# One hand-set order from w_out's last row tiles to w_up's first columns in a hybrid decoder layer on one Trainium2 core

## The chip, the cores and the metric

The kernel runs on one core of a Trainium2 chip. The metric is device time in microseconds of one execution, the median of several. The core has a matrix engine (TensorE, PE in the profile; PEld is its weight load), a vector engine (VectorE, DVE), a scalar engine (ScalarE, ACT), a GpSimd engine (POOL), and a queue engine (SyncE, SP) that issues most transfers. Each engine works through its own instructions in the order fixed when the kernel is built, and engines wait for one another by semaphores. Matmuls write to PSUM, eight banks of 128 partitions by 512 float32; the rest of the on-chip data lies in SBUF.

## The reference, cut to what matters

A decoder layer on 256 tokens with model width 2048, in float32:

```python
mix = hybrid_mixer(rmsnorm(h, norm_mix_pre), w_in, ..., w_out)   # ends in y_mix (256 x 4096) @ w_out
h = h + rmsnorm(mix, norm_mix_post)
ff = squared_relu_mlp(rmsnorm(h, norm_mlp_pre), w_up, w_down)    # relu(u @ w_up)^2 @ w_down
h = h + rmsnorm(ff, norm_mlp_post)
```

The place that the change touches is the seam of the two halves: the last products with w_out, the norm of their result over all 2048 columns, the residual sum, u of the second norm (transposed, since a matmul contracts over partitions), and the first 512 columns of u @ w_up.

## The kernel before, in words

**Tiles.** Tokens come in two tiles of 128 (t = 0 and 1), matrices in column blocks of 512 (NB). A weight tile is two blocks of 128 rows by 512 columns (KB = 2, 512 KB), and "k" counts such pairs: w_out has 16, w_up 8. Precision comes from splitting each float32 operand in two parts that the matmul takes: `split` (lines 132 to 138) makes hi on ACT (L135, or L137 with a scale for each row) and lo = source - hi on DVE (L136, L138). A product of row tiles is then three matmuls for each block of rows: hi times hi, hi times the weights' lo, lo times hi (L233 to L235). One weight tile on one tile of tokens is so six matmuls; the text calls that a row tile.

**Buffers.** `fetch` loads a weight tile through SP's queue into a ring of four raw buffers (RAWS); `parts` takes hi and lo from a ring of five (BUFS). `weights` fetches and splits ahead of the matmuls, at high priority. `fetch_next` also uses the place of u's second part, `ub`, as raw buffers while u isn't needed, and `in_place_of_u` lends that of the first, `ua`, to the sums of the seven-product scheme below.

**w_out.** y_mix @ w_out has four column blocks, n = 0 to 3, done in two units of two blocks (`unit`). Some pairs of k are done with seven products instead of eight (`seven`), whose sums `combine_new` puts together. What is left of the unit is plain row tiles, for the last four k (11, 13, 14, 15) first of block 2, both tiles of tokens for each k, then of block 3. In block 3 the tokens of t = 1 lag one k behind (LAG_OUT = 1). `mixed` takes a finished block from PSUM: adds it to what the sums gave (L804), squares it on ACT for the norm (L806), and multiplies by the norm's weights (L807). `done` does that for block 3 and puts `residual(t)` in the line of waiting work, from which `pump` takes a step between row tiles.

**The seam.** `residual` computes the norm's factor (`scale_of`: a sum on DVE, L766, and a power on POOL, L767), then for each of the four column blocks adds mw * factor to h (L817), transposes the block on PE in four pieces of 128 (L822) and splits the transposed pieces into u (L137 and L138). Then it squares h (L830) and computes the next norm's factor, rmlp. The first block of w_up is a plain product of row tiles (`gemm_tokens`, LAG_UP = 1, line 901), since the next norm's factor isn't known yet; `first_hidden` applies it afterwards. `over_partitions` (L491 to L493) spreads the factor for the other blocks of w_up, which are computed transposed (`gemm_features`, L333 and L336).

**Order.** Within an engine a list scheduler picks at build time, among the instructions that it holds ready in its own timeline, the one of highest priority; `tc.high_priority` raises it (weights by AHEAD, the residual's steps by twice that), otherwise what was written earlier goes first. `tc.manual_schedule` keeps the instructions written under it in that order on every engine. Kernel before uses it for the first product of the kernel (`first_block`, lines 425 to 470), at the highest priority; the squares of x (L423) numbered 5 to 7 are written behind that stretch.

Of the kernel before, what the change touches and what calls it, by code (L numbers as in the profile page):

```python
# [10 lines left out]
F32 = mybir.dt.float32  # L11
F32R = mybir.dt.float32r
BF16 = mybir.dt.bfloat16
# [3 lines left out]
P = 128  # L17
S = 256
# [24 lines left out]
AHEAD = 1_000_000  # L43
BUFS = 5
RAWS = 4
LAG_OUT = 1
LAG_UP = 1
LAG_DOWN = 3
WARM = 6
STAY = 4  # L50
# [23 lines left out]
def hymba_layer(ctx: ExitStack, tc: tile.TileContext, x, norm_mix_pre, w_in, conv_w, conv_b, dt_bias, a_log,  # L74
# [22 lines left out]
    def u(k):  # L97

        return us[k // SUMS][:, k % SUMS]
# [32 lines left out]
    def split(hi, lo, src, scale=None):  # L132

        if scale is None:
            return (nc.scalar.activation(hi, src, AF.Copy),  # L135
                    nc.vector.tensor_tensor(lo, src, hi.bitcast(F32), op=ALU.subtract))  # L136
        return (nc.scalar.activation(hi, src, AF.Copy, scale=scale),  # L137
                nc.vector.scalar_tensor_tensor(lo, src, scale, hi.bitcast(F32), op0=ALU.mult, op1=ALU.subtract))  # L138
# [49 lines left out]
    def weights(src, k0, c0, fetch=fetch):  # L188

        with tc.high_priority(offset=AHEAD):  # L190
            raw = fetch(src, k0, c0)
            hi, lo = parts()
            if fetch is fetch_next:
                split_in_line(hi, lo, raw)
                return hi, lo
            line.clear()
            with ExitStack() as order:
                while behind:
                    order.enter_context(tc.issue_after(behind.pop().ins))
                split(hi, lo, raw)  # L200
        return hi, lo
# [11 lines left out]
    def drain():  # L213
        while waiting:
            pump()

    def row_tiles(src, c0, ks, acc, acts, first=True, last=True, lag=0, at_end=None, pumps=1, fetch=fetch):


        held = {}  # L220
        n = len(ks)
        for i in range(n + lag):
            if i < n:
                held[i] = weights(src, ks[i] * KB, c0, fetch)
            for t, at in ((0, i), (1, i - lag)):
                if not 0 <= at < n:
                    continue
                hi, lo = held[at]
                ts = slice(t * P, (t + 1) * P)
                for j in range(KB):  # L230
                    a_h, a_l, r = acts(ks[at] * KB + j)
                    begin, end = first and at == 0 and j == 0, last and at == n - 1 and j == KB - 1
                    nc.tensor.matmul(acc[t], a_h[:, r, ts], hi[:, j], start=begin, stop=False)  # L233
                    nc.tensor.matmul(acc[t], a_h[:, r, ts], lo[:, j], start=False, stop=False)  # L234
                    nc.tensor.matmul(acc[t], a_l[:, r, ts], hi[:, j], start=False, stop=end)  # L235
                if at == n - 1 and at_end:
                    at_end(t, acc[t])
            pump(pumps)
# [68 lines left out]
    def unit(src, n, order, last, acc, more, combine, lag=0, at_end=(None, None), pumps=1, first=True):  # L307


        cols = (n * NB, (n + 1) * NB)  # L310
        sevens = [k for k, by_seven in order if by_seven]
        for i, (k, by_seven) in enumerate(order):
            if i + 1 < len(order) and order[i + 1][1]:
                sums_of_acts(order[i + 1][0])
            if by_seven:
                seven(src, *cols, k, acc, more, k == sevens[0], k == sevens[-1])
            else:
                for b in range(2):
                    row_tiles(src, cols[b], [k], acc[b::2], part, first and i == 0, False, pumps=pumps,
                              fetch=fetch_next)  # L320
            if k == sevens[-1]:
                combine(more)
        for b in range(2):
            row_tiles(src, cols[b], last, acc[b::2], part, False, True, lag if b else 0, at_end[b], pumps,
                      fetch=fetch if b else fetch_next)

    def features():
        return [bank().rearrange("p (b s) -> p b s", b=2) for _ in range(4)]
# [10 lines left out]
    def gemm_features(src, c0):  # L339


        acc = features()
        for k0 in range(0, NK, KB):
            hi, lo = weights(src, k0, c0)
# [419 lines left out]
    def scale_of(dst, sums, some, t):  # L764
        m = cp.tile([P, 1], F32, name="mean", bufs=2)
        nc.vector.tensor_scalar(m, sums[:, t, 3:4], some, 1.0 / D, op0=ALU.add, op1=ALU.mult)  # L766
        nc.gpsimd.tensor_tensor(dst[:, t:t + 1], m, half[:, 0:1], op=ALU.pow)  # L767
# [4 lines left out]
    def columns(n):  # L772
        return slice(n * NB, (n + 1) * NB)
# [25 lines left out]
            nc.vector.tensor_tensor(mw[:, 1, b], mw[:, 1, b], u, op=ALU.subtract)  # L799

    def mixed(n, t, acc):
        cs = columns(n)
        with tc.high_priority(offset=2 * AHEAD):
            nc.vector.tensor_tensor(mw[:, t, cs], acc, mw[:, t, cs], op=ALU.subtract if n % 2 else ALU.add)  # L804
            junk = hp.tile([P, NB], BF16, name="junk", bufs=2)
            nc.scalar.activation(junk, mw[:, t, cs], AF.Square, accum_out=ssq[:, t, n:n + 1])  # L806
            nc.vector.tensor_mul(mw[:, t, cs], mw[:, t, cs], wpost[n])  # L807

    def residual(t):

        ts = slice(t * P, (t + 1) * P)
        with tc.high_priority(offset=2 * AHEAD):
            scale_of(rm, ssq, first3[t], t)
        for n in range(4):
            cs = slice(n * NB, (n + 1) * NB)
            with tc.high_priority(offset=2 * AHEAD):
                nc.vector.scalar_tensor_tensor(h[:, t, cs], mw[:, t, cs], rm[:, t:t + 1], h[:, t, cs],  # L817
                                               op0=ALU.mult, op1=ALU.add)
                p = bank() if n % 2 else psmall()
                for f in range(4):  # L820
                    k = 4 * n + f
                    nc.tensor.transpose(p[:, f * P:(f + 1) * P], h[:, t, k * P:(k + 1) * P], ident)  # L822
                for f in range(4):
                    k = 4 * n + f
                    split(u(k)[:, 0, ts], u(k)[:, 1, ts], p[:, f * P:(f + 1) * P], w_mlp[:, k:k + 1])
            yield
        for n in range(4):
            cs = slice(n * NB, (n + 1) * NB)
            junk = hp.tile([P, NB], BF16, name="junk", bufs=2)
            nc.scalar.activation(junk, h[:, t, cs], AF.Square, accum_out=ssh[:, t, n:n + 1])  # L830
        scale_of(rmlp, ssh, sums_but_last(ssh, t), t)

    def done(t, acc):
        if t == 0:
            new_u()
        mixed(3, t, acc)
        waiting.append(residual(t))

    in_place_of_u()
    acc = [bank() for _ in range(2 * NT)]  # L840
# [20 lines left out]
    more = [psmall(), bank(), psmall(), bank()]  # L861

    def whole(n):
        return lambda t, a: mixed(n, t, a)

    def order_of(ks, by_seven):
        return [(k, k in by_seven) for k in ks]
# [4 lines left out]
        load_wpost(norm_mix_post, n)  # L872
    acc, more = more, acc

    def third(t, a):
        mixed(2, t, a)
        first3.append(sums_but_last(ssq, t))

    first3 = []
    unit(w_out, 2, order_of((0, 1, 6, 2, 9, 3, 12, 5, 4, 7, 8, 10), (6, 9, 12, 4, 8)), (11, 13, 14, 15), acc, more,  # L880
         lambda x: combine_new(2, x), LAG_OUT, (third, done), 2)


    def hidden(k, r):
        nc.scalar.activation(r, r, AF.Square)
# [96 lines left out]
```

## Time and profile before

| what | value |
|---|---|
| time, median of 3 runs | 1501.83 us (1501.44 to 1502.44) |
| time of the profiled execution | 1501.53 us |
| its span, first to last instruction | 1499.8 us |
| PE busy | 1483.3 us, 99% of the span, 7674 instructions |
| DVE busy | 1025.2 us, 68% |
| ACT busy | 795.9 us, 53% |
| POOL busy | 58.0 us, 4% |
| DMA | 283.15 MB, mean 189 GB/s |
| mean granted clock of PE | 0.998 |

A timeline row reads: start in us from the span's start, duration, engine, line, operation, what is written <- what is read, shapes and count; in brackets the idle time just before it and what ended that. A row with a count over 1 merges neighbours. Matmuls are pipelined, so one of 0.39 us can follow the one before after 0.23. Tile names: hi and lo are parts of weights; ah and al (attention), sh and sl (SSD) are the parts of y_mix; ua and ub those of u; acc and ps are PSUM; mw is the mixer's result, rmix the norm's factor, h the residual stream.

### The profile page before, as it was taken

How to read it: one execution, taken by the hardware profiler on the slowest of the kernel's cores; microseconds unless marked ns; L12 is line 12 of the kernel's file. 1: busy time of each engine (PE TensorE's matmuls, PEld its weight loads, DVE VectorE, ACT ScalarE, POOL GpSimd, SP SyncE). 2: the span in 40 equal slices, each digit the busy share in tenths (PEclk: the TensorE clock that was granted, in tenths of full speed). 3: DMA queues.
4: the chain of work that ended last, by engine and by line, in shares of the span. 5: the costliest groups of instructions: out<-in, count | busy, mean ns of one | idle time of the engine just before them, and what ended most of it. 6: DMA issues, size and time to landing. Idle time of an engine off the chain costs nothing.

```text
span 1499.8 us, 20349 instructions
## 1 busy us (share of the span) xinstructions
PE 1483.3 (99%) x7674; PEld 1267.0 (84%) x7674; DVE 1025.2 (68%) x1498; ACT 795.9 (53%) x1111; POOL 58.0 (4%) x73
## 2 busy tenths in 40 slices
PE   9999999999999999999989999999999999999997
PEld 8888888888888888888878888888888888888886
DVE  6988797886555565688977656644444665688886
ACT  7574665464545454555656545534444554555552
POOL 0002200220000000000000000000000000000101
PEclk9999999999999999999999999999999999999999
DMA  7665666555655655665555666555556666656662
GB/s 270 199 201 180 183 183 195 172 167 172 179 169 172 179 169 177 209 244 201 195 174 175 183 193 186 184 195 195 192 191 197 191 186 193 187 196 203 205 210 98
DMA packets 148707, 283.15 MB, mean 189 GB/s; under 512 B 11408, under 2 KB 14336, under 8 KB 148352
## 3 DMA queue, kind: packets, MB, share of 16 engines
q1 hardware_dynamic: 143312, 272.37, 58.3%
q10 hardware_dynamic: 5296, 9.48, 1.9%
q8 instruction: 60, 0.98, 0.3%
q14 instruction: 39, 0.32, 0.1%
HBM read 279.68 MB, written 2.13 MB: 188 GB/s over the span
## 4 chain that ended last, share of the span: by engine, by line
PE 94%; DVE 3%; DMA 2%; issue 1%; ACT 0%; SPq 0%; POOL 0%; POOLq 0%; DVEq 0%; ACTq 0%
PE acc L333 29%; PE acc L336 15%; PE acc L233 12%; PE acc L235 12%; PE acc L234 12%; PE ps L234 1%; PE ps L235 1%; PE ps L233 1%; PE acc L304 1%; PE acc L305 1%; PE acc L303 1%; DVE lo L136 1%; PE ps L654 1%; DMA raw<-in_w_in_dram 1%; PE ps L304 0%
## 5 line engine op out<-in xcount | busy, mean ns | idle before, releaser
L136 DVE TENSOR_TENSOR lo<-raw,hi 128x1024 fp32r<-128x1024 f32 (+1 forms) x466 | 570.7, 1226 | 395.1 <-ACT hi L135 392.7
L135 ACT ACTIVATE hi<-raw 128x1024 fp32r<-128x1024 f32 (+1 forms) x466 | 491.0, 1055 | 517.5 <-PE acc L333 240.5
L333 PE MATMUL acc<-ua,hi 128*128 128x512 f32 x1240 | 333.8, 399 | 0.7 <-DVE ua L138 0.7
L333 PEld LDWEIGHTS acc<-ua,hi 128*128 128x128 f32 x1240 | 217.8, 189 | 34.3 <-DVE ua L138 0.9
L333 PE MATMUL acc<-ub,hi 128*128 128x512 f32 x744 | 205.5, 397 | 0.0
L336 PEld LDWEIGHTS acc<-ua,lo 128*128 128x128 f32 x1240 | 182.0, 189 | 21.0
L336 PE MATMUL acc<-ua,lo 128*128 128x256 f32 x1240 | 187.3, 281 | 0.0
L333 PEld LDWEIGHTS acc<-ub,hi 128*128 128x128 f32 x744 | 127.3, 189 | 16.2 <-issue 0.2
L336 PEld LDWEIGHTS acc<-ub,lo 128*128 128x128 f32 x744 | 114.3, 189 | 15.8
L336 PE MATMUL acc<-ub,lo 128*128 128x256 f32 x744 | 118.2, 281 | 0.0
L233 PE MATMUL acc<-hi,sh 128*128 128x512 f32 x280 | 110.1, 393 | 0.0
L235 PE MATMUL acc<-hi,sl 128*128 128x512 f32 x280 | 109.1, 390 | 0.0
L234 PE MATMUL acc<-lo,sh 128*128 128x512 f32 x280 | 109.1, 390 | 0.0
L233 PE MATMUL acc<-hi,ah 128*128 128x512 f32 x264 | 102.8, 389 | 0.0
L235 PE MATMUL acc<-hi,al 128*128 128x512 f32 x264 | 102.8, 389 | 0.0
L234 PE MATMUL acc<-lo,ah 128*128 128x512 f32 x264 | 102.8, 389 | 0.0
L233 PE MATMUL acc<-hi,ua 128*128 128x512 f32 x180 | 71.3, 396 | 0.3 <-ACT ua L137 0.3
L235 PE MATMUL acc<-hi,ua 128*128 128x512 f32 x180 | 70.2, 392 | 0.4 <-DVE ua L138 0.4
L234 PE MATMUL acc<-lo,ua 128*128 128x512 f32 x180 | 70.4, 391 | 0.0
L135 ACT ACTIVATE hi<-ub 128x1024 fp32r<-128x1024 f32 x48 | 50.4, 1058 | 37.5 <-PE acc L235 13.6
L136 DVE TENSOR_TENSOR lo<-ub,hi 128x1024 fp32r<-128x1024 f32 x48 | 58.3, 1222 | 12.1 <-ACT hi L135 11.5
L235 PEld LDWEIGHTS acc<-hi,sl 128*128 128x128 f32 x280 | 52.6, 188 | 11.0
(300 smaller groups left out, 1903.9 us busy)
## 6 DMA issues: line engine op xcount, KB each, us to landing
raw<-in_w_in_dram SPq DMA_DIRECT2D x190, 512.0 KB, 3.6
raw<-in_w_up_dram SPq DMA_DIRECT2D x128, 512.0 KB, 3.8
raw<-in_w_down_dram SPq DMA_DIRECT2D x104, 512.0 KB, 4.3
raw<-in_w_out_dram SPq DMA_DIRECT2D x40, 512.0 KB, 4.2
ub<-in_w_out_dram SPq DMA_DIRECT2D x24, 512.0 KB, 4.6
ub<-in_w_down_dram SPq DMA_DIRECT2D x24, 512.0 KB, 5.0
bc<-acs_d ACTq DMA_DIRECT2D x8, 512.0 KB, 4.4
xs<-in_x_dram SPq DMA_DIRECT2D x8, 256.0 KB, 6.4
```

Source lines behind the costliest of these rows:

```text
L135: return (nc.scalar.activation(hi, src, AF.Copy), nc.vector.tensor_tensor(lo, src, hi.bitcast(F32), op=ALU.subtract))
L136: nc.vector.tensor_tensor(lo, src, hi.bitcast(F32), op=ALU.subtract))
L233: nc.tensor.matmul(acc[t], a_h[:, r, ts], hi[:, j], start=begin, stop=False)
L234: nc.tensor.matmul(acc[t], a_h[:, r, ts], lo[:, j], start=False, stop=False)
L235: nc.tensor.matmul(acc[t], a_l[:, r, ts], hi[:, j], start=False, stop=end)
L303: nc.tensor.matmul(dst, a_h, hi[:, j], start=own and first, stop=False)
L304: nc.tensor.matmul(dst, a_h, lo[:, j], start=False, stop=False)
L305: nc.tensor.matmul(dst, a_l, hi[:, j], start=False, stop=own and last)
L333: nc.tensor.matmul(acc[f], hi[:, j, f * P:(f + 1) * P], u(k0 + j), start=k0 + j == 0, stop=False, skip_group_check=True)
L336: nc.tensor.matmul(acc[f][:, 0], lo[:, j, f * P:(f + 1) * P], u(k0 + j)[:, 0], start=False, stop=k0 + j == NK - 1, skip_group_check=True)
L654: nc.tensor.matmul(p[:, c, r], bc[:, r, c * P:(c + 1) * P], xdt[:, c, r], start=True, stop=True)
```

## The change

The last four k of w_out's block 3, everything of the seam, the first column block of w_up and the first weight tile of its second block become one stretch, `mix_to_up`, written instruction group by instruction group under `tc.manual_schedule()` at priority AHEAD. It is called from `unit` in place of the last row tiles. Inside it:

- `out(t, i)` is a row tile of w_out, `rows(t, i)` one of w_up; all four of w_out for t = 0 come ahead of those of t = 1, and t = 0 of w_up is three row tiles ahead before t = 1 begins.
- w_out's third and fourth weight tile are split into the place of `ua`, which the sums no longer need, instead of into the ring of five. u takes that place once the last `out` is done.
- The parts of `mixed` and `residual` are steps of their own: `mix` (was L804), `mix_square` (L806), `weight` (L807), `add` (L817), `turn` (L822, now spread over two banks), `take` (the splits into u, two k at a time), `square` (L830). `weight` of block 3 writes to a tile of its own.
- `weigh(i)` loads and splits a tile of w_up; `weigh(8)` is the next block's first, which `gemm_features` is handed as `begun`.

LAG_OUT, LAG_UP, `third`, `done`, `residual`, the `gemm_tokens` call for w_up, `drain` and the parameter `pumps` of `unit` go. `row_tile` is the inner loop of `row_tiles` as a function.

```diff
+    def mix_to_up(c0, ks, acc):
+        up = [bank() for _ in range(NT)]
+        banks, turned = [], {}
+        weighed = hp.tile([P, NT, NB], F32, name="e")
+        room_w = big.tile([P, SUMS, 2, S], F32R, name="ua").rearrange("p k b s -> p k (b s)")
+        def tile_of(src, k, c0, at=None):
+            raw = fetch(src, k * KB, c0)
+            hi, lo = parts() if at is None else (room_w[:, at + KB * i:at + KB * (i + 1)] for i in range(2))
+            split(hi, lo, raw)
+            return hi, lo
...
+        o, w = {}, {}
+        with tc.high_priority(offset=AHEAD), tc.manual_schedule():
+            o[0] = tile_of(w_out, ks[0], c0)
+            out(0, 0)
+            o[1] = tile_of(w_out, ks[1], c0)
+            out(0, 1)
+            o[2] = tile_of(w_out, ks[2], c0, 0)
+            o[3] = tile_of(w_out, ks[3], c0, 4)
+            mix(0, 2)
+            mix_square(0, 2)
+            out(0, 2)
+            mix(1, 2)
+            mix_square(1, 2)
+            first3[0] = sums_but_last(ssq, 0)
+            first3[1] = sums_but_last(ssq, 1)
+            out(0, 3)
+            mix(0, 3)
+            weight(0, 2)
+            weigh(0)
+            out(1, 0)
+            mix_square(0, 3)
+            out(1, 1)
+            scale_of(rm, ssq, first3[0], 0)
+            weigh(1)
+            add(0, 0)
+            out(1, 2)
+            add(0, 1)
+            turn(0, 0)
+            weigh(2)
+            square(0, 0)
+            out(1, 3)
+            new_u()
+            take(0, 0)
+            square(0, 1)
+            mix(1, 3)
+            turn(0, 1)
+            take(0, 1)
+            take(0, 2)
+            rows(0, 0)
+            mix_square(1, 3)
+            rows(0, 1)
+            scale_of(rm, ssq, first3[1], 1)
+            add(0, 2)
+            take(0, 3)
+            add(1, 0)
+            weigh(3)
+            square(0, 2)
+            weight(1, 3)
+            rows(0, 2)
+            add(1, 1)
+            square(1, 0)
+            turn(1, 0)
+            turn(0, 2)
+            take(1, 0)
+            rows(0, 3)
+            take(0, 4)
+            take(1, 1)
+            turn(1, 1)
+            rows(1, 0)
+            square(1, 1)
+            rows(1, 1)
+            weight(1, 2)
+            take(1, 2)
+            add(1, 2)
+            weigh(4)
+            turn(1, 2)
+            add(1, 3)
+            take(0, 5)
+            take(1, 3)
+            rows(1, 2)
+            rows(0, 4)
+            turn(1, 3)
+            square(1, 2)
+            weight(0, 3)
+            add(0, 3)
+            take(1, 4)
+            rows(1, 3)
+            weigh(5)
+            take(1, 5)
+            weigh(6)
+            turn(0, 3)
+            rows(1, 4)
+            rows(0, 5)
+            take(1, 6)
+            square(0, 3)
+            weigh(7)
+            take(0, 6)
+            rows(1, 5)
+            take(0, 7)
+            square(1, 3)
+            rows(1, 6)
+            scale_of(rmlp, ssh, sums_but_last(ssh, 0), 0)
+            rows(0, 6)
+            weigh(8)
+            take(1, 7)
+            rows(0, 7)
+            rows(1, 7)
+            scale_of(rmlp, ssh, sums_but_last(ssh, 1), 1)
+        for t in range(NT):
+            waiting.append(first_hidden(t, up[t]))
+        pump(NT)
+        return w[8]
...
-    acc = gemm_tokens(w_up, 0, act_u, NK, LAG_UP, None, 2)
-    drain()
-    for t in range(NT):
-        waiting.append(first_hidden(t, acc[t]))
+    unit(w_out, 2, order_of((0, 1, 6, 2, 9, 3, 12, 5, 4, 7, 8, 10), (6, 9, 12, 4, 8)), (11, 13, 14, 15), acc, more,
+         lambda x: combine_new(2, x), ending=mix_to_up)
+    begun = ended.pop()
     over_partitions(rbc, rmlp)
...
-            acc = gemm_features(w_up, hf * 4096 + fb * NB)
+            acc = gemm_features(w_up, hf * 4096 + fb * NB, begun)
+            begun = None
```

More of the change, by code (lines that the diff above doesn't have):

```diff
@@ L45 @@
 RAWS = 4
-LAG_OUT = 1
-LAG_UP = 1
 LAG_DOWN = 3
@@ L215, in drain, with row_tile @@
             pump()
+    def row_tile(dst, t, parts, k0, acts, begin, end):
+        hi, lo = parts
+        ts = slice(t * P, (t + 1) * P)
+        for j in range(KB):
+            a_h, a_l, r = acts(k0 * KB + j)
+            nc.tensor.matmul(dst, a_h[:, r, ts], hi[:, j], start=begin and j == 0, stop=False)
+            nc.tensor.matmul(dst, a_h[:, r, ts], lo[:, j], start=False, stop=False)
+            nc.tensor.matmul(dst, a_l[:, r, ts], hi[:, j], start=False, stop=end and j == KB - 1)
     def row_tiles(src, c0, ks, acc, acts, first=True, last=True, lag=0, at_end=None, pumps=1, fetch=fetch):
@@ L227, in row_tiles @@
                     continue
[L228 to L235, printed above, removed]
+                row_tile(acc[t], t, held[at], ks[at], acts, first and at == 0, last and at == n - 1)
                 if at == n - 1 and at_end:
@@ L305, in seven, with unit @@
             nc.tensor.matmul(dst, a_l, hi[:, j], start=False, stop=own and last)
-    def unit(src, n, order, last, acc, more, combine, lag=0, at_end=(None, None), pumps=1, first=True):
+    def unit(src, n, order, last, acc, more, combine, lag=0, at_end=(None, None), first=True, ending=None):
         cols = (n * NB, (n + 1) * NB)
@@ L318, in unit @@
                 for b in range(2):
-                    row_tiles(src, cols[b], [k], acc[b::2], part, first and i == 0, False, pumps=pumps,
+                    row_tiles(src, cols[b], [k], acc[b::2], part, first and i == 0, False,
                               fetch=fetch_next)
@@ L323, in unit @@
         for b in range(2):
-            row_tiles(src, cols[b], last, acc[b::2], part, False, True, lag if b else 0, at_end[b], pumps,
-                      fetch=fetch if b else fetch_next)
+            if b and ending:
+                ended.append(ending(cols[b], last, acc))
+            else:
+                row_tiles(src, cols[b], last, acc[b::2], part, False, True, lag if b else 0, at_end[b],
+                          fetch=fetch if b else fetch_next)
     def features():
@@ L863, in whole, with at_end @@
     def whole(n):
-        return lambda t, a: mixed(n, t, a)
+        def at_end(t, a):
+            with tc.high_priority(offset=2 * AHEAD):
+                mixed(n, t, a)
+        return at_end
     def order_of(ks, by_seven):
@@ L873, in hymba_layer @@
     acc, more = more, acc
[L875 to L881, printed above, removed]
+    first3 = {}
+    ended = []
     def hidden(k, r):
```

68 lines of the change are left out of this document (37 added, 31 removed).

## The prediction

> **What bounds the kernel now.** I read the page first, for the engine that has no room. The rows give busy time, share of the span and count.
>
> ```profile
> span 1499.8 us, 20349 instructions
> PE 1483.3 (99%) x7674; PEld 1267.0 (84%) x7674; DVE 1025.2 (68%) x1498; ACT 795.9 (53%) x1111; POOL 58.0 (4%) x73
> ```
>
> TensorE is busy 1483.3 of 1499.8 us, so only time in which it stands still, or runs its matmuls further apart than it could, can be won. I then asked for PE's waits in the stage that the change touches, 735 to 850 us (total, times, longest):
>
> ```profile
> PE ps L822 <- DVE h L817: 3.2, 1, 3.2
> PE acc L235 <- DVE ua L138: 0.4, 1, 0.4
> PE acc L233 <- ACT ua L137: 0.3, 1, 0.3
> ```
>
> One wait of 3.2 us for the residual, two small ones for u. The timeline of the same stage shows what leads up to it:
>
> ```profile
> 766.34 0.39 PE L233 MATMUL ps<-hi,ah 128*128 128x512 f32 x1
> ...
> 768.38 0.39 PE L233 MATMUL acc<-hi,ah 128*128 128x512 f32 x1
> ...
> 777.66 0.68 DVE L804 TENSOR_TENSOR mw<-acc,mw 128x512 f32<-128x512 f32 x1
> ...
> 781.11 0.68 DVE L804 TENSOR_TENSOR mw<-acc,mw 128x512 f32<-128x512 f32 x1
> 781.27 0.55 POOL L767 TENSOR_TENSOR rmix<-mean,half 128x1 f32<-128x1 f32 x1 [442.13 <-DVE mean L766]
> 781.85 2.08 DVE L817 SCALAR_TENSOR_TENSOR h<-mw,rmix,h 128x512 f32<-128x512 f32 x3
> 781.88 0.63 ACT L806 ACTIVATE junk<-mw 128x512 bf16<-128x512 f32 x1 [1.12 <-DVE mw L804]
> ...
> 782.66 0.66 PE L822 MATMUL ps<-cst,h 128*128 128x128 f32 x4 [3.24 <-DVE h L817]
> ...
> 783.35 0.37 ACT L137 ACTIVATE ua<-ps,par 128x128 fp32r<-128x128 f32 x1
> ...
> 783.77 0.50 PE L233 MATMUL acc<-hi,ua 128*128 128x512 f32 x1
> ...
> 810.58 0.60 PE L492 MATMUL ps<-dg,ones 128*128 128x128 f32 x4
> ```
>
> From 766.34 to 768.38 lie nine matmuls: 0.2267 us each, 1.36 us for a row tile of six. At 768.38 the last four k of w_out's column block 3 begin; at 810.58 the first w_up block is over. Between them, 42.20 us, PE has 24 row tiles (8 of w_out, 16 of w_up), 32.64 us, and eight sets of four transposes. What these cost, and how close DVE's instructions follow one another, the next rows give:
>
> ```profile
> 785.65 0.68 DVE L807 TENSOR_TENSOR mw<-mw,wpost 128x512 f32<-128x512 f32 x1
> ...
> 786.25 0.34 DVE L138 SCALAR_TENSOR_TENSOR ua<-ps,par,ua 128x128 fp32r<-128x128 f32 x1
> ...
> 786.51 0.34 DVE L138 SCALAR_TENSOR_TENSOR ua<-acc,par,ua 128x128 fp32r<-128x128 f32 x1
> ...
> 786.77 0.74 DVE L817 SCALAR_TENSOR_TENSOR h<-mw,rmix,h 128x512 f32<-128x512 f32 x1
> ...
> 787.43 0.34 DVE L138 SCALAR_TENSOR_TENSOR ua<-ps,par,ua 128x128 fp32r<-128x128 f32 x1
> ...
> 787.56 0.66 PE L822 MATMUL acc<-cst,h 128*128 128x128 f32 x4
> ...
> 787.98 0.48 PE L234 MATMUL acc<-lo,ua 128*128 128x512 f32 x1
> ...
> 796.22 1.22 DVE L136 TENSOR_TENSOR lo<-raw,hi 128x1024 fp32r<-128x1024 f32 x1
> ...
> 797.35 0.35 DVE L138 SCALAR_TENSOR_TENSOR ua<-ps,par,ua 128x128 fp32r<-128x128 f32 x1
> ```
>
> A set of transposes holds PE 0.42 us (787.56 to 787.98), eight 3.36. So 42.20 - 32.64 - 3.36 = **6.20 us** of the stage are lost: 3.24 as the plain wait, the rest in rows that start late one by one. DVE's pitch is 0.60 us for a 512-wide mix or weight, 0.26 for a 128-wide take, 0.66 for a residual add, 1.13 for the lo half of a weight tile. An add's start to its transposes is 0.79 to 0.81 us, transposes to the first take 0.69, a take on ACT to its row matmul 0.42.
>
> **The change, part by part.** No matmul, transpose or byte goes or comes; order and places do. What I count is when each engine's queue lets PE go on, from 0 at 768.38, with all engines in the written order and w_out's block 2 done before it (the rival below drops this).
>
> Tokens 0, w_out: four row tiles, 0 to 5.44. The last matmul lands at 5.21 + 0.39. The mix starts at 5.65; before, it was issued at 777.66, 9.28 on this scale, since a tile of the other tokens came between and a lo half lay ahead of it. Behind it on DVE: weight(0,2) 6.25, lo of w0 6.85, the mean 7.99, lo of w1 8.12, add(0,0) 9.26, add(0,1) 9.92. ACT's square starts 0.77 after the mix (781.11 to 781.88) and POOL's power takes 0.58 to the add, so neither is late. Transposes can start at 9.26 + 0.79 = 10.05. Meanwhile three row tiles of tokens 1 run to 9.52: **wait 0.53**.
>
> Transposes, then out(1,3), end at 10.05 + 0.42 + 1.36 = 11.83. The first take writes u into the place that held two of w_out's tiles, so it waits for that row tile's last write, 0.16 us after its slot, and reaches ACT at about 12.1; the first w_up row starts at 12.52, after transposes that end at 12.25: **0.27**. Behind that added wait stand, on ACT, a square and the next takes, on DVE mix(1,3) and the takes; I count them all after it. Three rows of tokens 0 run to 16.60. DVE does mix(1,3) 13.02, four takes from 13.62, the second mean 14.98 (ACT's square releases it), add(0,2) 15.1, two takes 15.77, add(1,0) 16.29. Its transposes start 17.08: **0.48**. Two sets of transposes end at 17.92; row (0,3) needs lo of w3, which ends 18.19: **0.15**. Row ends 19.43; transposes wait for add(1,1) at 18.70 + 0.79: **0.06**. Rows (1,0), (1,1) end 22.63; add(1,2) at 22.05 + 0.79: **0.21**. From there DVE runs ahead: lo of w5 is done at 28.59 for a row at 29.54, the last takes at 34.95 for a row at 36.34. I find no later wait.
>
> Sum: 32.64 + 3.36 + 1.70 = 37.70 us against 42.20: **4.50 us less**. If transposes closed up to nothing and no wait stayed, 42.20 - 32.64 = 9.56 would be the bound of all gain, and with transposes as they are, 6.20.
>
> Moved transfers: the four w_out and nine w_up loads of the block keep their order on SP, ahead of those of the next block. One load lands in about 4 us:
>
> ```profile
> raw<-in_w_up_dram SPq DMA_DIRECT2D x128, 512.0 KB, 3.8
> ```
>
> With four raw buffers w4's load waits for lo of w0 (8.0), so it lands near 12 and is split near 21; w8's waits for w4's (23.9), lands near 28, is split near 30. Free, with 2 us in hand; without that cover each missing us is a us of PE. The ninth tile w8 is split early and handed on; w9, behind the block's last instructions on DVE, has its lo near 36.5, and the next block reaches it at about 41. Free too. The loads of the last norm's weights on ACT's queue wait for the weight steps' buffers (the last at 25.6) and are needed only in w_down. The two first_hidden steps, rmlp and over_partitions follow the last row; rmlp's second power ends near 35.9, before PE needs it.
>
> **The rivals.**
>
> (1) *DVE becomes the bound.* The row of the stage, busy us of PE, PEld, DVE, ACT, POOL, then granted clock and DMA:
>
> ```profile
> 768.38:810.58 42.20, 38.20 (x177) 29.87 (x176) 34.10 (x75) 28.71 (x69) 3.06 (x4) 1.00 0.50 152
> ```
>
> My walk has DVE without a pause from 5.65 to 35.2: some 63 instructions at their closest pitch. Nothing else may slip in, and in before the takes do wait for ACT. At 0.04 us more each, DVE ends 2.5 us later, of which 1.4 are slack at the end. Early waits grow likewise: 2.0 to 2.5 us of the gain go, 1499.7. For: DVE's 34.10 of 42.20. Against: the pitches are of the same instructions, mixed.
>
> (2) *PE takes the new tiles ahead of older ones* (ends slower). The block carries a higher priority than the rows of w_out's block 2 that precede it, and its tiles are split well before those rows run:
>
> ```profile
> 757.50 0.39 PE L233 MATMUL ps<-hi,ah 128*128 128x512 f32 x1
> 757.70 1.06 ACT L135 ACTIVATE hi<-raw 128x1024 fp32r<-128x1024 f32 x1 [1.65 <-PE acc L235]
> ...
> 758.79 1.23 DVE L136 TENSOR_TENSOR lo<-raw,hi 128x1024 fp32r<-128x1024 f32 x1 [0.54 <-ACT hi L135]
> ```
>
> At 757.50 block 2's last four k begin; the first tile of block 3 is split by 760.02. If the ordering lets it in there, PE runs seven row tiles of block 3 first, and block 2 ends only at 777.55. mix(1,2) starts at 777.76, and behind it in the fixed order stand the sums (ACT's square, to 779.50), mix(0,3), weight 780.10, lo of w0 780.70, mean 781.84, lo of w1, add(0,0) 783.12; transposes 783.91, 5.48 after my 778.43. 4.50 less, 5.48 more: 1502.8, and PE stands still 6.36 us at one place. With three tiles ahead the delay is about 0.4 us, each further one costs its 1.36; from the sixth on the gain is gone, which is where this rival decides. Against it: kernel before has a hand-ordered stretch at its start, and ACT's queue there shows
>
> ```profile
> 21.80 0.60 PE L414 MATMUL ps<-cst,xs 128*128 128x128 f32 x4
> ...
> 26.80 1.06 ACT L135 ACTIVATE hi<-raw 128x1024 fp32r<-128x1024 f32 x1
> 28.70 0.84 ACT L137 ACTIVATE ub<-ps,par 128x256 fp32r<-128x256 f32 x2 [0.84 <-PE ps L414]
> 29.42 0.63 ACT L423 ACTIVATE junk<-xs 128x512 bf16<-128x512 f32 x1
> ...
> 31.93 0.62 ACT L423 ACTIVATE junk<-xs 128x512 bf16<-128x512 f32 x1
> ```
>
> a 0.84 us gap ahead of 28.70 in which the square of 31.93, from outside the stretch, would have fitted; its input had been transposed with the columns of 21.80. It was not let in, which speaks for a stretch that keeps strangers out.
>
> (3) *The same, with a slowed clock.* In before PE's 3.24 us gap cost nothing beyond itself: granted clock 1.00 in the row of the stage. If after 6.36 us of standing the clock were half for as long as that harmless gap, 14 matmuls would take 0.2267 more each, 3.2 us: 1506.0; half of it 1504.4. The Trainium skill's page "TensorE: Matmul & The Clock Gate", Part 1, says that an idle window of about 3.4 us halves the clock; the gap here of 3.24 is just under it, so the 1.00 agrees and no run here shows more.
>
> (4) *It gives the gain back in the next block*: with one tile split ahead instead of several, a late w9 stops PE there, up to the 4 us of one load: about 1501.
>
> **How the numbers follow.** The profiled execution took 1501.53 us, 0.30 under the median 1501.83. 1501.53 - 4.50 = 1497.03, on the median's scale **1497.3**. A measurement of this kernel tells about 0.2%, 3.0 us, from no change. Forecast, 1495.6 (6.2 us) to 1498.8: 0.54. Rival 1, 1498.8 to 1501.3: 0.17, same. Rival 2, 1501.5 to 1505: 0.17, of it 0.10 same and 0.07 slower. Rival 3: 0.07, slower. Rival 4: 0.05, 0.03 same and 0.02 slower. Faster 0.54, same 0.30, slower 0.16. The range 1495.6 to 1503.5 takes in the forecast, rivals 1 and 4 and the larger part of rival 2; the forecast's own is 1495.6 to 1498.8.
>
> **What would show it.** Right: the first w_out matmul of block 3 after the last of block 2; mix about 5.7 us after it; first w_up row near 12.5 and the last ending near 37.7 us after it; PE's waits there in pieces under 0.6 us, for adds. Wrong by rival 1: the pieces grow and name lo or u late in the stage. By rival 2: block 3's matmuls stand between block 2's, and one wait over 5 us names h. By rival 3: clock below 1.00 after it. By rival 4: the wait lies in the next block and names hi or lo.

## The result and the profile after

The kernel after takes 1506.13 us (median of 12, 1505.35 to 1507.04) against 1501.43 us for the kernel before (median of 12, 1500.69 to 1504.69): a ratio of 1.003, with a 95% interval of 1.0022 to 1.0037. It is slower by 4.7 us, outside the predicted range, and at the time of rival 3.

The page of the kernel after, read as that of before:

```profile
span 1504.1 us, 20339 instructions
PE 1485.0 (99%) x7674; PEld 1267.5 (84%) x7674; DVE 1025.1 (68%) x1498; ACT 795.1 (53%) x1111; POOL 58.2 (4%) x73
```

The work is the same; the span grew by 4.3 us, PE's busy time by 1.7. So most of the loss is standstill, and a part of it is matmuls that took longer. PE's waits from 735 to 850 us (total, times, longest) say where:

```profile
PE ps L858 <- DVE h L849: 6.7, 1, 6.7
PE acc L858 <- DVE h L849: 0.2, 1, 0.2
PE ps L496 <- DVE dg L495: 0.2, 1, 0.2
```

One wait of 6.7 us for the residual stands where before had 3.2. All others together are 0.4 us: past this place the new order does keep PE fed. PE's timeline in the kernel after shows how the wait arises:

```profile
757.70 0.39 PE L221 MATMUL ps<-hi,ah 128*128 128x512 f32 x1
...
759.06 0.45 PE L221 MATMUL acc<-hi,ah 128*128 128x512 f32 x1
759.35 0.39 PE L221 MATMUL ps<-hi,ah 128*128 128x512 f32 x1
...
765.86 0.39 PE L221 MATMUL acc<-ua,ah 128*128 128x512 f32 x1
...
778.35 0.39 PE L223 MATMUL ps<-hi,al 128*128 128x512 f32 x1
785.46 1.11 PE L858 MATMUL ps<-cst,h 128*128 128x128 f32 x4 [6.73 <-DVE h L849]
...
788.50 0.39 PE L223 MATMUL acc<-ua,al 128*128 128x512 f32 x1
788.73 0.60 PE L858 MATMUL acc<-cst,h 128*128 128x128 f32 x4
```

In these rows of w_out, ps stands for the two banks of column block 2 (tokens 0 and 1) and acc for those of block 3, so "hi,ah" with acc or "ua,ah" is a row tile of block 3 (its third and fourth weight tile lie in ua). Block 2's last four k begin at 757.70. At 759.06, one row tile later, a matmul of block 3 stands between them, and from there the two are mixed. Block 2's last matmul comes at 778.35, and it is also the last thing that PE has: seven of block 3's eight row tiles are done by then, the eighth stands behind the transposes in the written order. What PE waits for is the chain on DVE and POOL:

```profile
777.41 0.69 DVE L838 TENSOR_TENSOR mw<-ps,mw 128x512 f32<-128x512 f32 x1 [10.63 <-PE ps L223]
778.77 0.69 DVE L838 TENSOR_TENSOR mw<-ps,mw 128x512 f32<-128x512 f32 x1 [0.67 <-PE ps L223]
...
782.84 0.21 DVE L770 TENSOR_SCALAR mean<-ssq,some 128x1 f32<-128x1 f32 x1
782.99 1.23 DVE L134 TENSOR_TENSOR lo<-raw,hi 128x1024 fp32r<-128x1024 f32 x1
783.13 1.49 POOL L771 TENSOR_TENSOR rmix<-mean,half 128x1 f32<-128x1 f32 x1 [443.82 <-DVE mean L770]
784.65 1.42 DVE L849 SCALAR_TENSOR_TENSOR h<-mw,rmix,h 128x512 f32<-128x512 f32 x2 [0.44 <-POOL rmix L771]
```

DVE's queue stands still for 10.63 us until block 2's sums of products are there for the mix of 777.41 (tokens 0; that of tokens 1 is at 778.77), while everything that PE will need is queued behind that mix. After the wait PE is slow as well. Stretches of the kernel after (busy us of PE, PEld, DVE, ACT, POOL, granted clock, DMA share, GB/s):

```profile
768.60:778.60 10.00, 10.00 (x45) 8.07 (x43) 0.69 (x1) 0.46 (x1) 0.00 (x0) 1.00 0.19 72
778.60:788.73 10.13, 3.40 (x11) 2.71 (x11) 7.38 (x13) 5.27 (x11) 1.49 (x1) 0.66 0.38 109
788.73:800.00 11.27, 11.02 (x56) 8.40 (x55) 10.41 (x26) 10.09 (x32) 0.99 (x1) 1.00 0.29 89
```

and the same place in the kernel before, its gap and what follows:

```profile
779.40:782.66 3.26, 0.02 (x2) 0.01 (x1) 3.20 (x6) 2.08 (x5) 0.55 (x1) 1.00 0.72 204
782.66:784.00 1.34, 1.33 (x9) 1.04 (x10) 1.34 (x4) 1.30 (x4) 0.00 (x0) 1.00 0.60 231
```

The clock is at 1.00 up to the gap and again from 788.73. In between PE issues four transposes and six matmuls, from 785.46 to 788.73: 3.27 us, where by the prediction's prices 0.42 + 6 x 0.2267 = 1.78 would do. In e1 and e3 below, at a clock of 1.00, the same ten take 1.89 and 1.88. So the slowed clock costs about 1.4 us here.

To compare kernels I use the length of the **seam**: from the first matmul of block 2's last four k to the first read of a finished sum of the next block by ACT. It leaves out what varies in the 750 us ahead, where this start moves between 757 and 760 us. The end rows of before and of after:

```profile
832.36 0.39 ACT L356 ACTIVATE r<-acc 128x256 f32<-128x256 f32 x1 [0.59 <-PE acc L336]
```

```profile
836.97 0.39 ACT L360 ACTIVATE r<-acc 128x256 f32<-128x256 f32 x1 [0.59 <-PE acc L340]
```

Before: 832.36 - 757.50 = 74.86 us. After: 836.97 - 757.70 = 79.27, 4.41 more, which is nearly the whole 4.7 of the medians. The first transposes cut the seam in two: 25.16 us up to them and 49.70 from them in before, 27.76 and 51.51 in after. Ratios in the table are to runs of before on the same chip.

| kernel | seam, us | against before, us | time, us | ratio to before, 95% |
|---|---|---|---|---|
| before | 74.86 | | 1501.43 | |
| after | 79.27 | +4.41 | 1506.13 | 1.003 (1.0022 to 1.0037) |
| e1_block2_first | 71.68 | -3.18 | 1498.83 | 0.9978 (0.9968 to 0.9987) |
| e2_no_priority | 71.71 | -3.15 | 1499.21 | 0.9979 (0.997 to 0.9988) |
| e3_fill_gap | 78.02 | +3.16 | 1504.94 | 1.0019 (1.001 to 1.0028) |
| e4_four_ahead | 75.08 | +0.22 | 1501.82 | 0.9997 (0.9988 to 1.0006) |
| e5_before_longer_gap | 75.88 | +1.02 | 1503.76 | 1.0011 (1.0002 to 1.002) |
| e8_block2_first_again | 71.71 | -3.15 | 1498.94 | 0.9986 (0.9977 to 0.9995) |
| e6_power_alone | 70.74 | -4.12 | 1497.41 | 0.997 (0.9958 to 0.9981) |
| e7_both_powers | 71.64 | -3.22 | 1497.95 | 0.9974 (0.9964 to 0.9984) |

### The profile page after: what moved, and what is told of

Its sections match the earlier page's. It is cut to its first block, busy times and chain, and to the rows that moved or that the text cites. A ratio compares the mean times of both kernels' runs of the same rounds, so it can differ in the third digit from the quotient of the medians.

```text
span 1504.1 us, 20339 instructions
## 1 busy us (share of the span) xinstructions
PE 1485.0 (99%) x7674; PEld 1267.5 (84%) x7674; DVE 1025.1 (68%) x1498; ACT 795.1 (53%) x1111; POOL 58.2 (4%) x73
## 4 chain that ended last, share of the span: by engine, by line
PE 94%; DVE 3%; DMA 2%; issue 1%; ACT 1%; SPq 0%; POOL 0%; POOLq 0%; DVEq 0%; ACTq 0%
PE acc L337 29%; PE acc L340 15%; PE acc L222 12%; PE acc L221 12%; PE acc L223 12%; PE ps L222 1%; PE ps L223 1%; PE ps L221 1%; PE acc L305 1%; DVE lo L134 1%; PE acc L306 1%; PE acc L304 1%; PE ps L658 1%; DMA raw<-in_w_in_dram 1%; PE ps L305 0%
## 5 line engine op out<-in xcount | busy, mean ns | idle before, releaser
L337 PE MATMUL acc<-ua,hi 128*128 128x512 f32 x1240 | 334.0, 399 | 0.2 <-DVE ua L136 0.2
L337 PEld LDWEIGHTS acc<-ua,hi 128*128 128x128 f32 x1240 | 217.6, 189 | 34.0 <-DVE ua L136 0.4
L337 PE MATMUL acc<-ub,hi 128*128 128x512 f32 x744 | 205.5, 397 | 0.0
L337 PEld LDWEIGHTS acc<-ub,hi 128*128 128x128 f32 x744 | 127.2, 189 | 16.3 <-issue 0.2
L221 PE MATMUL acc<-hi,ah 128*128 128x512 f32 x256 | 99.7, 390 | 0.0
L223 PE MATMUL acc<-hi,al 128*128 128x512 f32 x256 | 99.6, 389 | 0.0
```

What stands on the lines that cost most here:

```text
L221: nc.tensor.matmul(dst, a_h[:, r, ts], hi[:, j], start=begin and j == 0, stop=False)
L223: nc.tensor.matmul(dst, a_l[:, r, ts], hi[:, j], start=False, stop=end and j == KB - 1)
L337: nc.tensor.matmul(acc[f], hi[:, j, f * P:(f + 1) * P], u(k0 + j), start=k0 + j == 0, stop=False, skip_group_check=True)
```

## The experiments

The theory after the result: the whole loss comes from the order in which PE takes the row tiles at the entry, once as a longer wait and once more as a slowed clock. The rival to it: something inside the stretch is dear (its fixed order, its places in ua, DVE's load), and the entry is only where it shows.

**Block 2 first (e1).** One ordering edge is added: block 3's first matmul is issued after block 2's last. Nothing else differs from the kernel after.

```diff
+    newest = [None]
...
-            nc.tensor.matmul(dst, a_l[:, r, ts], hi[:, j], start=False, stop=end and j == KB - 1)
+            newest[0] = nc.tensor.matmul(dst, a_l[:, r, ts], hi[:, j], start=False, stop=end and j == KB - 1)
...
-            out(0, 0)
+            with tc.issue_after(newest[0].ins):
+                out(0, 0)
```

> The changed kernel with one more ordering edge: the stretch's first w_out matmul is issued after the last matmul of block 2. Theory A (seven tiles of block 3 jumped ahead, and the long standstill slowed the clock): block 2 is done first, no wait over 1 us for h in the stage, clock 1.00 throughout, and the forecast's time, 1497.3 us, that is 4 to 5 us under the kernel before (1501.4). Theory B (DVE's queue in the fixed order is the bound whatever PE does first): many waits remain, 1500 to 1504.

Measured: 1498.83 us, ratio 0.9978 (0.9968 to 0.9987). The one edge moves the seam by 7.59 us against after (79.27 to 71.68), and the sign of the change with it. Rows of PE, POOL, DVE and ACT in e1:

```profile
759.10 0.39 PE L223 MATMUL ps<-hi,ah 128*128 128x512 f32 x1
...
778.25 1.49 POOL L773 TENSOR_TENSOR rmix<-mean,half 128x1 f32<-128x1 f32 x1 [437.56 <-DVE mean L772]
...
779.78 1.41 DVE L851 SCALAR_TENSOR_TENSOR h<-mw,rmix,h 128x512 f32<-128x512 f32 x2 [0.44 <-POOL rmix L773]
...
780.59 0.66 PE L860 MATMUL ps<-cst,h 128*128 128x128 f32 x4 [0.92 <-DVE h L851]
...
830.78 0.39 ACT L362 ACTIVATE r<-acc 128x256 f32<-128x256 f32 x1 [0.59 <-PE acc L342]
```

```profile
768.00:790.00 22.00, 20.84 (x98) 16.45 (x96) 14.84 (x30) 12.44 (x32) 2.48 (x2) 1.00 0.36 112
```

The wait is 0.92 us, and the second fence, the window over it, has the clock at 1.00. Up to the transposes e1 needs 21.49 us, 6.27 less than after: 6.73 - 0.92 = 5.81 is wait, the other 0.46 lies in the mixed row tiles, which run a little further apart (759.06 to 759.35 in after is 0.29, not 0.2267). Behind them it needs 50.19, 1.32 less, which is the clock's 1.4 but for some hundredths. The entry is the cause; the inside of the stretch works. But the gain is 3.2 and not 4.5, and POOL's power took 1.49 us where the sum had 0.55 to 0.58.

**No priority (e2).** Is it the priority, or would an ordered stretch mix in anyway, since its tiles are ready early?

```diff
-        with tc.high_priority(offset=AHEAD), tc.manual_schedule():
+        with tc.manual_schedule():
```

> The changed kernel, with the raised priority of the stretch taken away and nothing else. Theory A: priority alone let the tiles jump, so this comes close to the run with the ordering edge, 1497 to 1499, plus what splits of the next block cost when they come between on DVE. Theory B': the written order itself put the tiles first, and it stays at 1506.

Measured: 1499.21 us, ratio 0.9979 (0.997 to 0.9988), the seam 0.03 us from e1's. PE's row at the place of the wait in e2:

```profile
780.61 0.65 PE L858 MATMUL ps<-cst,h 128*128 128x128 f32 x4 [0.92 <-DVE h L849]
```

Without the priority the older rows go first by themselves. The priority alone let block 3 in front.

**The gap filled (e3).** 28 needless matmuls, issued after block 2's last, keep PE busy while it waits; they write to a bank that is not yet in use (`block2` holds block 2's last matmul). If the clock falls because PE stands still, the 1.5 us must come back while the wait's own length stays lost.

```diff
+        def fill(n):
+            a_h, a_l, r = part(ks[3] * KB)
+            for _ in range(n):
+                nc.tensor.matmul(up[0], a_h[:, r, 0:P], o[3][0][:, 0], start=True, stop=True)
...
+        block2 = newest[0]
...
             out(1, 2)
+            with tc.issue_after(block2.ins):
+                fill(28)
             add(0, 1)
```

> The changed kernel with 28 needless matmuls (6.35 us, written into a bank that is not yet in use) put behind block 2's last, where PE stands still for 6.7 us. Theory A: the order stays as it is, the standstill shrinks to about 0.4 us, the granted clock stays at 1.00, and what the slow clock cost goes: the transposes and six matmuls behind the gap took 3.27 us instead of 1.78, so 1.5 us less, 1504.6. If the clock is no cause: 1506.1 as before.

Measured: 1504.94 us, ratio 1.0019 (1.001 to 1.0028); seam 1.25 us shorter than after's. Stretches in e3, up to the transposes (which now wait 0.39 us) and behind them:

```profile
778.60:786.20 7.60, 7.21 (x33) 5.64 (x31) 5.88 (x13) 5.02 (x9) 1.49 (x1) 1.00 0.19 46
786.20:790.00 3.80, 3.78 (x20) 3.02 (x21) 3.06 (x6) 2.46 (x9) 0.00 (x0) 1.00 0.74 227
```

The clock column is 1.00 in both. PE's row of the transposes and ACT's at the end of the seam in e3:

```profile
786.19 0.66 PE L860 MATMUL ps<-cst,h 128*128 128x128 f32 x4 [0.39 <-DVE h L851]
...
836.49 0.39 ACT L362 ACTIVATE r<-acc 128x256 f32<-128x256 f32 x1 [0.59 <-PE acc L342]
```

Up to the transposes e3 needs 27.72 us (its seam begins at 758.47), as after does (27.76): the delay is the same. Behind them it needs 836.49 - 786.19 = 50.30, 1.21 less than after and near e1's 50.19. That is what the fallen clock costs in the end.

**Four ahead (e4).** The edge of e1 is moved from block 3's first row tile to its fifth: four may overtake. By the prediction's rival 2, each further tile ahead costs its length.

```diff
-            out(1, 0)
+            with tc.issue_after(block2.ins):
+                out(1, 0)
```

> As the first run, but the edge holds back only the fifth row tile of block 3 (first of tokens 1), so that four go ahead of block 2's end instead of seven. Theory A: delay 0.4 + 1.36 us against the run with none ahead by the prediction's count, so about 1.8 us above it (near 1499), standstill under 3 us and clock 1.00. If jumping tiles were harmless and something else costs, it lies at 1506.

Measured: 1501.82 us, ratio 0.9997 (0.9988 to 1.0006), not told from before. PE's row at the transposes and three stretches, the gap and what follows it, in e4:

```profile
782.31 0.67 PE L860 MATMUL ps<-cst,h 128*128 128x128 f32 x4 [2.65 <-DVE h L851]
```

```profile
779.60:782.30 2.70, 0.06 (x1) 0.00 (x0) 2.26 (x5) 1.15 (x2) 1.49 (x1) 1.00 0.48 119
782.30:784.00 1.70, 1.69 (x7) 1.47 (x8) 1.70 (x2) 0.72 (x2) 0.00 (x0) 0.65 0.98 340
784.00:785.40 1.40, 1.40 (x5) 0.94 (x4) 0.06 (x1) 0.00 (x0) 0.00 (x0) 0.50 0.53 130
```

The delay is as the mechanism has it: the wait is 2.65 - 0.92 = 1.73 us longer than e1's. Up to the transposes e4 needs 23.68 us (its seam begins at 758.63), 2.19 more than e1 (the wait, and again 0.46 in the mixed rows). Behind them, though, it needs 51.40, 1.21 more than e1, because the clock fell to 0.65 and 0.50 behind a gap of 2.65 us. In all e4's seam is 3.40 us longer than e1's, where I had expected 1.8 and a clock of 1.00, on the ground that before's 3.24 us left it alone. That ground is wrong.

**Before with a longer gap (e5).** The kernel before, with a chain of copies and powers on POOL behind the factor of tokens 0, meant to lengthen its wait. Does its clock fall then, and what does that cost in the old order?

```diff
             scale_of(rm, ssq, first3[t], t)
+            if t == 0:
+                m = cp.tile([P, 1], F32, name="mean", bufs=2)
+                nc.gpsimd.tensor_copy(m, rm[:, 0:1])
+                for _ in range(2):
+                    nc.gpsimd.tensor_tensor(m, m, half[:, 0:1], op=ALU.pow)
+                    nc.gpsimd.tensor_tensor(m, m, half[:, 0:1], op=ALU.pow)
+                nc.gpsimd.tensor_copy(rm[:, 0:1], rm[:, 0:1])
```

> The kernel before with six needless GpSimd instructions behind the power that gives tokens 0 their factor (0.55 us each by the power's row, so about 3.3 us), which lengthens PE's 3.24 us gap to about 6.5 us and changes nothing else. If a standstill of that length slows the clock, the granted clock behind it falls below 1.00 and the time grows by the gap's growth and some 1.5 us more, about 4.8 us (1506.2). If the clock does not follow the gap: by 3.3 us (1504.7).

Measured: 1503.76 us, ratio 1.0011 (1.0002 to 1.002). Rows of POOL, of PE at the transposes and of ACT at the end of the seam, and the stretches of the gap and behind it, in e5:

```profile
784.93 0.18 POOL L820 COPY rmix<-rmix 128x1 f32<-128x1 f32 x1
785.07 0.54 POOL L819 TENSOR_TENSOR mean<-mean,half 128x1 f32<-128x1 f32 x1
...
785.96 1.11 PE L829 MATMUL ps<-cst,h 128*128 128x128 f32 x4 [4.25 <-DVE h L824]
...
835.66 0.39 ACT L356 ACTIVATE r<-acc 128x256 f32<-128x256 f32 x1 [0.59 <-PE acc L336]
```

```profile
781.70:785.96 4.26, 0.01 (x2) 0.01 (x1) 3.18 (x6) 2.07 (x5) 2.19 (x6) 0.94 0.72 226
785.96:789.30 3.34, 3.34 (x15) 3.03 (x16) 3.04 (x7) 2.92 (x10) 1.46 (x3) 0.56 0.01 2
```

The gap grew by 1.0 us only, to 4.25, because the edit did less than I meant: the last copy reads only the factor and not the chain, so the list scheduler put it (784.93) ahead of three of the four powers, and the adds waited for no more than that. The clock fell all the same (0.56), but from the transposes on e5 needs 835.66 - 785.96 = 49.70 us, exactly what before needs, and the seam grew by the gap's 1.02 alone. In before the rows behind the transposes start late one by one anyway, as the prediction's sum of 6.20 us has it, and slow matmuls fill that time. So a fallen clock is not always dear. In after it was: PE had a row tile ready behind the transposes.

**Block 2 first, again (e8), and the power moved (e6).** e1's gain was 1.3 us short of the sum, with POOL's power at 1.49 us. In e1 it runs beside the lo half of w1 on DVE. e6 is e1 with that split put behind the adds; e8 is e1 once more, as its neighbour. The rival theory was that a power after 440 idle us is slow by itself.

```diff
             scale_of(rm, ssq, first3[0], 0)
-            weigh(1)
             add(0, 0)
             out(1, 2)
             add(0, 1)
+            weigh(1)
             turn(0, 0)
```

> The run with the ordering edge once more, as the neighbour of the two that follow: 3 to 4 us under the kernel before, GpSimd's first power 1.49 us as then.

> The run with the ordering edge, and w1's split moved behind the two residual adds on DVE, so that no DVE instruction runs beside GpSimd's power for tokens 0. Theory A: the power took 1.49 us instead of 0.55 because DVE's SBUF-to-SBUF subtraction ran beside it; it takes 0.55 now, PE's first wait falls from 0.92 to about 0.1, and the time by 0.8 us against the neighbour. Theory B: the power was slow after 440 us without work on GpSimd: it stays at 1.49, the adds wait as before, and the time stays.

Measured: e8 1498.94 us, ratio 0.9986 (0.9977 to 0.9995); e6 **1497.41 us, ratio 0.997 (0.9958 to 0.9981)**, the lowest median of all (its interval overlaps those of e8 and e7, so the comparison with them goes by the seam). Rows of POOL, PE and ACT in e6:

```profile
757.41 0.39 PE L223 MATMUL ps<-hi,ah 128*128 128x512 f32 x1
...
776.57 0.55 POOL L773 TENSOR_TENSOR rmix<-mean,half 128x1 f32<-128x1 f32 x1 [437.53 <-DVE mean L772]
...
777.96 0.66 PE L860 MATMUL ps<-cst,h 128*128 128x128 f32 x4
...
783.24 0.99 POOL L773 TENSOR_TENSOR rmix<-mean,half 128x1 f32<-128x1 f32 x1 [6.13 <-DVE mean L772]
...
828.15 0.38 ACT L362 ACTIVATE r<-acc 128x256 f32<-128x256 f32 x1 [0.59 <-PE acc L342]
```

Its bracket still shows 437.53 idle us, and the power takes 0.55: it was the neighbour on DVE, not the rest. PE's wait is gone from the row of 777.96, and the seam is 0.97 us shorter than e8's. Nearly all of it lies ahead of the transposes: 20.55 us up to them where e8 has 21.49, and 50.19 from them against 50.22. Not all of that is the power's doing, since the move takes the split out of the adds' way on DVE as well. In e1 the add comes 1.81 us behind the mean, with the split done and DVE waiting for the power at the end; the prediction had 1.28 with the split between them, e6 has 0.87 without it. So about 0.5 us is the longer power, the rest the split.

**Both powers (e7).** The second power still takes 0.99 us beside an add. e7 is e6 with that add behind the takes and w3's split, and with the transposes that need it behind a row tile.

```diff
-            add(0, 2)
             take(0, 3)
             add(1, 0)
             weigh(3)
+            add(0, 2)
...
             turn(1, 0)
-            turn(0, 2)
             take(1, 0)
             rows(0, 3)
+            turn(0, 2)
```

> As the run before it, and the residual add of tokens 0, block 2 moved away from the second power, behind the takes, the add of tokens 1 and w3's split; its transposes move behind w_up's fourth row tile. Theory A: the second power takes 0.55 instead of 0.99, the second pause of PE (0.6 us before the transposes of tokens 1) shrinks to about 0.2, 0.3 to 0.4 us less than the run before it, and no new wait. Theory B: second power and time unchanged.

Measured: 1497.95 us, ratio 0.9974 (0.9964 to 0.9984), the seam 0.90 longer than e6's. The power's row and PE's at its new wait in e7:

```profile
783.29 0.55 POOL L773 TENSOR_TENSOR rmix<-mean,half 128x1 f32<-128x1 f32 x1 [6.13 <-DVE mean L772]
...
791.64 0.66 PE L860 MATMUL acc<-cst,h 128*128 128x128 f32 x4 [0.42 <-DVE h L851]
```

The power is at 0.55, as expected, and nothing is won: nobody had waited for it. The moved add is late for ACT, whose square of it starts at 786.53 (784.24 in e6); the takes behind that square come late, DVE stands idle for 0.46 us before the one of 788.15, and PE waits 0.42 for the next add of tokens 1. The rest of the 0.90 is not taken apart. The move was a miss; a short instruction is only worth what waits for it.

## Why the prediction was wrong, point by point

**The step that failed** is the condition of the walk, "w_out's block 2 done before it", and the argument that held rival 2 down to 0.17: "a stretch that keeps strangers out". I had read it from a gap of 0.84 us on ACT in the kernel's first stretch, which an older square did not fill. The runs show no such fence. At the entry the priority decides among the ready matmuls (e1 and e2 each turn it round), and at the end of the stretch instructions from outside slip in, as rows of DVE and PE in the kernel after show:

```profile
811.73 4.62 DVE L134 TENSOR_TENSOR lo<-raw,hi 128x1024 fp32r<-128x1024 f32 x4
813.43 0.61 PE L337 MATMUL acc<-ua,hi 128*128 128x512 f32 x2
816.27 0.60 DVE L136 SCALAR_TENSOR_TENSOR ub<-ps,par,ub 128x128 fp32r<-128x128 f32 x2
```

The four splits of 811.73 and the matmuls of L337 belong to the next column block, and the take of 816.27, which is in the stretch, comes behind them. Why the square stayed out of the first stretch was not tried.

**Rival 2's chain** was right in kind, step by step. mix(1,2) was forecast at 777.76 and came at 778.77: 0.20 of the 1.01 is the seam's later start (757.70 against 757.50), 0.46 the mixed rows, which the forecast had at the full pace, and 0.35 a slip in it, since seven row tiles from 768.38 end at 777.90 and not 777.55. The stand of 6.36 us came as 6.73. The transposes, forecast at 783.91, came at 785.46, 1.55 later: the 1.01, and 0.53 between mean and add (782.84 to 784.65, 1.81 in place of 1.28), where the power beside the split of w1 held DVE up.

**Rival 3's mechanism** was right and its size half: the slow time behind the gap lasted some 3 us, not the 6.3 of 14 matmuls at half speed, and cost 1.2 to 1.4 us in place of 3.2. That its total of 1506.0 meets the 1506.13 is partly luck: the walk gave -3.18 (not -4.50), the displacement 6.27 (not 5.48, for the 0.35 and the 0.46 above) and the clock 1.32 (not 3.2), together the seam's 4.41.

**The walk**, with its condition restored, was right in kind. e1 and e2 gain 3.2 us where it gave 4.50. Two terms were mis-sized. Up to the transposes the sum had 14.28 (768.38 to 782.66) - 10.05 = 4.23 less than before, and e1 has 25.16 - 21.49 = 3.67: 0.56 missing, 0.53 of it the same longer way from mean to add; e6, with the split no longer between them, has 4.61. Behind the transposes the sum had 0.27 less, and e1 and e6 need 50.19 - 49.70 = 0.49 more: 0.76 missing. Most of that is a cost that I had left out, of going from transposes to row matmuls: in e1 the first matmul behind a set is followed after 0.32 us instead of 0.2267, in six of the eight places, 0.55 us in all, as these rows of PE in e1 show for the first set (the matmul behind the transposes of 780.59 and the one after it, 781.00 to 781.32):

```profile
781.00 0.48 PE L223 MATMUL acc<-ua,ah 128*128 128x512 f32 x1
781.32 0.40 PE L224 MATMUL acc<-ua,ah 128*128 128x512 f32 x1
```

The rest is not taken apart.

**Rival 1** (DVE the bound) did not come: past the entry PE's waits in after sum to 0.4 us, and none names lo or u. **Rival 4** did not come either: the ninth tile handed on was enough, with no wait for w9. The DMAs that were costed at nothing cost nothing that PE's waits show.

**The range** ended at 1503.5 because I gave rivals 2 and 3 together 0.24, and set the bound within rival 2. The evidence against rival 2 was one gap whose cause I had not established; the evidence for it was in two quoted rows (tiles split by 760.02, older rows running to 768) and in the code, where a higher priority is all that the order among ready instructions depends on.

## What to carry to other kernels

Ordering a stretch by hand fixes the order within it, not against what was written before it: if it also gets a higher priority, its first ready matmuls overtake older ones that others wait for, and one ordering edge (or no priority) is worth more than the whole arrangement behind it, here 7.6 us. When an engine's order is changed, ask first what the first waiting instruction of each queue waits for, and whether that still runs first. A standstill of PE of some us can be paid twice, by its length and by a slowed clock behind it; and a tiny instruction on which all wait belongs beside nothing that it can be blocked by.

## What the runs showed of the hardware

**The clock has no safe gap at three us.** It fell after gaps of 2.65 (e4), 4.25 (e5) and 6.73 us (after), but in the profiled execution of before not after 3.24. Read in stretches of 0.1 us, the granted clock there is 1.00 or 0.50, but for the stretches in which it changes. It stays at 0.50 for 3.41 us in e4 (782.82 to 786.24) and in e5 (785.48 to 788.89), and for twice that, 6.83, in after (781.66 to 788.48). In e4 it fell when PE had been at work again for 0.51 us; of the 3.41 us up to the fall PE was busy for 0.76. That fits a clock that is set every 3.41 us by how busy PE was in the stretch just past, so that a gap's place counts as well as its length; this is inferred from three falls, and where those stretches lay in before no run shows.

That execution of before was not typical. The mean granted clock of a whole execution is 0.998 or 0.999 in 55 of the 57 of e1, e2, e3, e6, e7 and e8, in which PE's waits here are under 1 us (the two others, 0.996 and 0.997, are of e8 and took 3.7 and 4.1 us longer than its median, so a gap here is not the only thing that lowers the mean); 0.994 to 0.996 in all 12 of after; and for before, among the 31 that stood beside e1 to e4, it is 0.996 or 0.997 in 22. So the 3.24 us gap probably costs clock in most executions, though only profiled ones show where. Before's times are hardly longer where the mean is lower (medians of 1502.36 at 0.996, 1501.94 at 0.997 and 1501.82 at 0.998, each with a spread of 2 to 3 us), which agrees with e5: slow matmuls there lie in time that is waited out anyway. The Trainium skill's page "TensorE: Matmul & The Clock Gate", Part 1, says that the window of about 3.4 us is free-running, so that the phase decides; the stays of 3.41 us and the spread over executions agree with that, while the fall in e4 shows that PE need not have been idle for a whole window.

**POOL's 128x1 power** takes 0.55 us alone (e6) or beside an instruction that reads PSUM (a mix in before, a take in e7's second), 1.49 beside a lo split and 0.99 beside a residual add. In the slow cases it ends 0.4 us after that DVE instruction: in after the split ends at 782.99 + 1.23 = 784.22, the power at 784.62. So what it costs depends on how much of that instruction is left: two powers of e5 that began later in a residual add took 0.62 and 0.58. The Trainium skill's page "SBUF — State Buffer", section "Who interferes with whom", says that a DVE instruction with two SBUF inputs contends with a GpSimd instruction that reads SBUF, and calls the port pair that they share an exclusive lock; both slow neighbours have two SBUF inputs, the harmless mix and take have one beside PSUM, and the ends agree with a lock. The reverse, a power that holds up DVE, no run here shows.
